# Differential attention: turning the weights of three pairs of heads by the DMA crossbar instead of by TensorE

## The chip, the cores and the metric

One Trainium2 chip; the kernel runs on one core. The metric is the device time of one execution in microseconds (us), as the median of several runs. The engines are named as in the profile: PE is TensorE (PEld its weight load), DVE VectorE, ACT ScalarE, POOL GpSimd, SP SyncE, which here issues the loads of weights.

## The reference

A hybrid decoder layer for 256 tokens of width 1024: a SwiGLU block, then a Mamba-2 branch and a branch of differential attention side by side, merged by gates, then a second SwiGLU block. What matters here is the attention, 8 heads in 2 blocks of 128 queries:

```
s = einsum('bqhmd,bkhmd->bhmqk', q_blk, k) * scale - slopes * dist      # m: two maps a head
s = where(dist >= 0, s, -inf)
p = softmax(s, axis=-1)
attn = p[:, :, 0] - lam * p[:, :, 1]
out = einsum('bhqk,bkhe->bqhe', attn, v)
out = rmsnorm(out, subln_g) * (1.0 - lam_init)
```

`attn` stands with the queries on the partitions. For the product with the values the keys have to be there, so each head's weights (three blocks of 128x128: the first queries with the first keys, the second queries with both) have to be turned.

## The kernel before

Float32 matmuls are made of a rounded part and its remainder: each 1 MB chunk of weights is loaded by SP into one of three buffers `raw`; ACT rounds it (`whi`, line 357, two halves a chunk) and DVE makes the remainder (`wlo`, line 358); when both halves are done, SP loads the next chunk into the buffer. PE multiplies whi and wlo with the tokens. Its order is written out by hand in this part: `natural` runs the products of the gates (`pgt`), of the Mamba-2 branch (`pws`) and of the attention (`pwd`) in blocks of 12 or 24 matmuls, and between two blocks lets a piece of `att_work` in, a generator that is measured out by microseconds and stops at each BREAK. The PSUM banks of these products (`pj`) are three that take turns; line 1847 (gates) or 1856 (`pws`) on DVE empties them. What stands on ACT and DVE is put in order by the scheduler, one row for each engine, worked off in that order.

`att_work` goes by waves of two heads, a pair. Wave n makes the scores of pair n on PE (`psc`), adds the distances on DVE (`s`, line 1625), takes the maximum (`nm`), exponentials on ACT (line 513, four a head) and combines the two maps on DVE (line 1647). In the same wave the pair before, n - 1, is turned: `Head.turn` puts three transposes a head on PE (`pa`, line 1653) and one copy on ACT (`aT`, line 1655). Then `values` multiplies aT with the values (`po`, lines 1665 to 1667), and `Pair.norm` makes the square (`o`, line 1679, ACT), its sum on DVE (`ro`, lines 1681 and 1682), its power by Ln and Exp on ACT, and the product (`o`, line 1686, DVE). A pair's result is turned a wave or so later (`pto`, line 1692, PE; `oh`, line 1704, ACT). Behind the third pair's softmax the gates' sigmoids (`gt`) stand on ACT between two loads of a table.

The tiles `s` come from a pool of four buffers (`k3`), `aT` and `o` from one of seven (`k2`). The second SwiGLU block already turns two tiles by DMA (`by_dma`, lines 1083 to 1090): ACT copies the low and the high 16 bits of each float apart, a DMA issued from ACT turns both planes, and ACT puts the halves together again.

Of the kernel before, what the change touches and what calls it, by code (L numbers as in the profile page):

```python
# [18 lines left out]
U16 = mybir.dt.uint16  # L19
# [8 lines left out]
P = 128  # L28
# [20 lines left out]
SSD_US = 1.55  # L49
DOWN = {"f1": "q1 Q2 q3 Q0 ppp", "f2": "q1 Q2 q3 Q0 ppp"}  # L50
DMA_TURNS = ("f2",)
WIDE_Z = ((0, 0), (1, 0), (1, 1))
FIRST, LAST = (1, 2, 3, 5, 7, 6, 4), (1, 6, 7, 2, 3, 5, 4)
MIXED = (1, 2, 6, 5, 3, 7, 4)
# [4 lines left out]
def tile_hybrid_layer(ctx: ExitStack, tc: tile.TileContext, x, ffn1_pre_g, ffn1_w_gate, ffn1_w_up,  # L59
# [4 lines left out]
    nc = tc.nc  # L64
# [8 lines left out]
    def k3(shape, name, dt=F32):  # L73
        return sb.tile(shape, dt, tag="k3", name=name, bufs=K3_BUFS)

    def k2(shape, name, dt=F32):
        return sb.tile(shape, dt, tag="k2", name=name, bufs=K2_BUFS)
# [15 lines left out]
    def bg(shape, name):  # L93
        return ps.tile(shape, F32, tag="bg", name=name, bufs=5)


    class Quad:
# [6 lines left out]
        def __init__(self, i, products, homes=None):  # L104
            self.i, self.sums, self.products, self.homes = i, {}, products, homes
            self.uses = [[p for p in products if p in (1, 5)], [p for p in products if p in (5, 7)],
                         [p for p in products if p in (2, 4)], [p for p in products if p in (3, 6, 7)]]
# [296 lines left out]
    def take(ahead=AHEAD):  # L404

        i = taken[0]
        taken[0] += 1
        split_to(ahead_of(i, ahead))
        (of, p), w = units[i], splits[i]
        splits[i] = None  # L410
        if p is not None:
            return w
        his, los = w
        nj = chunks[of][1][1] // 2
        return (lambda j: his[j // nj][:, j % nj, :], lambda j: los[j // nj][:, j % nj, :])
# [37 lines left out]
    def mm_w(dst, name, w, act, scale=None):  # L453

        for m in range(2):
            acc = pj(f"{name}{m}")
            for part in PARTS[m]:
                mm_part(acc, w, act, m, part, part == PARTS[m][0])
            taken_from(acc, dst[:, m, :], scale)

    def mm_runs(dst, name, w, act, n, wide=True):


        banks = [pj(f"{name}{m}") if n % 2 == 0 or not wide else bg([P, 512], f"{name}{m}") for m in range(2)]
        for part in PARTS[n % 2]:
            for m, acc in enumerate(banks):
                mm_part(acc, w, act, m, part, part == PARTS[n % 2][0])
                if part == PARTS[n % 2][1]:
                    taken_from(acc, dst[:, m, :])
# [69 lines left out]
    h = const.tile([P, 2, D], F32, name="h")  # L539
# [44 lines left out]
    for name, v in (("mx", mix_pre_g), ("f2", ffn2_pre_g),  # L584
                    ("ng", ssd_norm_g), ("cb", ssd_conv_b), ("sg", da_subln_g)):
        n = v.shape[1] // P
# [43 lines left out]
    def turn(b, q, src, g, to, name):  # L630

        pu = transposed(b, q, src, name)
        gained(pu, q, g, *to(q))
        return pu
# [195 lines left out]
    def sums_of(g, even, odd):  # L830


        bs = (slice(0, P), slice(P, T))
        v = k4([P, 4, 2, P], f"sv{g}")
        full = g in (0, 3)
        hi, lo = ((k4 if full else k3)([P, 4 if full else 3, 2, P], f"s{n}{g}", F32R) for n in "hl")
        more = None if full else k2([P, 2, 2, P], f"s4{g}", F32R)
        nc.vector.tensor_tensor(v[:, 0], even[:, :, bs[1]], odd[:, :, bs[1]], ALU.add)
        nc.vector.tensor_sub(v[:, 2], even[:, :, bs[0]], even[:, :, bs[1]])
        nc.vector.tensor_sub(v[:, 1], v[:, 0], even[:, :, bs[0]])  # L840
        nc.vector.tensor_sub(v[:, 3], odd[:, :, bs[0]], v[:, 1])
        if full:
            split(hi, lo, v)
            return tuple([x_[:, i] for i in range(4)] for x_ in (hi, lo))
        split(hi, lo, v[:, 0:3])
        split(more[:, 0], more[:, 1], v[:, 3])
        return ([hi[:, i] for i in range(3)] + [more[:, 0]], [lo[:, i] for i in range(3)] + [more[:, 1]])
# [127 lines left out]
    class Norm:  # L975
# [16 lines left out]
        def turn0(self, q):  # L992
            self.pus.append(turn(0, q, h[:, 0, halves[q]], self.g, self.to0, self.tag))
# [14 lines left out]
        def turn1(self, q):  # L1008
            turn(1, q, self.un[q], self.g, in_u(1), self.tag)
# [44 lines left out]
    def ffn(post_v, tag, ready, turned, then, products):  # L1054
# [50 lines left out]
        for j in range(2, FF // T):  # L1105
# [6 lines left out]
            mm_runs(sg, f"pg_{tag}{j}", take(), act_u, 0)  # L1112
            if tag in DMA_TURNS and j in (2, 3):
                for t in turns:
                    next(t)
            if j == 2:
                if tag not in DMA_TURNS:
                    for b in range(2):
# [10 lines left out]
            if j // 2 in QUADS[tag]:  # L1129
                if j % 2:  # L1130
                    sums[j // 2] = sums_of(j // 2, even, sg)
                else:
                    even = sg
            if first and (j == 3 or tag not in DMA_TURNS):
                sums[0] = sums_of(0, first[0][:, :2, :], first[0][:, 2:, :])
# [465 lines left out]
    ol = [None] * 2  # L1601
    blk = (slice(0, P), slice(P, 3 * P))

    class Head:


# [41 lines left out]

        def turn(self):

            pa = bg([P, 3 * P], f"pa{self.hd}")
            for i3 in range(3):
                nc.tensor.transpose(pa[:, i3 * P:(i3 + 1) * P], self.s[:, 0, i3 * P:(i3 + 1) * P], ident)
            self.aT = k2([P, 3 * P], f"aT{self.hd}")
            nc.scalar.copy(self.aT, pa)
            self.s = None

# [10 lines left out]

    class Pair:


        def __init__(self, hp):
            self.hp = hp
# [35 lines left out]
    def att_work():  # L1709

        pairs = [Pair(hp) for hp in range(H_ATT // 2)]
        heads = [Head(hd, pairs[hd // 2]) for hd in range(H_ATT)]
        for n in range(H_ATT // 2 + 2):
            here, old = heads[2 * n:2 * n + 2], heads[2 * n - 2:2 * n] if n else []
            for head in here:
                head.scores()
            for head in here:
                head.softmax()  # L1720
                yield 2.3
            for head in old:
                head.turn()
            if n == 3:
                pairs[0].turn()
                yield 0.8
            if old and opens:
                opens.pop()()
            for head in here:
                head.combine()  # L1730
                yield 1.3
            yield BREAK
            if old:
                for head in old:
                    head.values()
                pairs[n - 1].norm()
                if n == 4:
                    pairs[2].turn()
                yield 1.8
            if n == 5:  # L1740
                yield BREAK
            if n in (3, 5):
                pairs[n - 2].turn()
                yield 0.8
# [39 lines left out]
    for g in range(4):  # L1784
        sz[g] = k4([P, 4, T], f"sz{g}")
        for i in range(2):
            dst = sz[g][:, i * 2:i * 2 + 2, :]
            if (g, i) in WIDE_Z:
                mm_w(dst, f"pz{g}{i}", take(), act_u)
# [10 lines left out]
    for c in range(4):  # L1800
# [7 lines left out]
        back.run(QK_US)  # L1808

    back.add(att_work())  # L1810


# [148 lines left out]
```

## Time and profile before

| | |
|---|---|
| time, median of 3 runs | 723.69 us (723.62 to 723.75) |
| the profiled execution | 723.79 us, its span 722.1 us |
| busy PE, DVE, ACT | 99%, 89%, 68% of the span |
| granted TensorE clock | 0.998 |

Times in the profile are microseconds from the start of the span. "x6" is a count of instructions, and in brackets stands the idle time of the engine ahead of the row with what ended it. A chain of work is followed back from the last instruction over what released each one. The rows of a stretch give the busy time of each engine.

### The profile page before, as it was taken

To read this page: it belongs to the slowest core of one execution; us is meant where nothing else is said; L and a number is where in the kernel's file an instruction comes from. 1 tells how busy PE (TensorE), PEld (TensorE's weight loads), DVE (VectorE), ACT (ScalarE), POOL (GpSimd) and SP (SyncE) were. 2 spreads that over 40 slices of the span, in tenths; PEclk is the share of its full clock that TensorE was granted. 3 is DMA by queue.
4 is the path that set the end of the run, shared out by engine and by line. 5 is a ranking of instruction groups with operands and counts; after the bars stand their busy time and mean duration, and the time that the engine had idled before them with its cause. 6 is when DMAs were issued, how large, how long until landed. Compare 5 with 4: busy or idle time off the path is not lost.

```text
span 722.1 us, 10617 instructions
## 1 busy us (share of the span) xinstructions
PE 714.0 (99%) x3933; PEld 613.1 (85%) x3933; DVE 642.9 (89%) x994; ACT 489.5 (68%) x831; POOL 60.8 (8%) x110
## 2 busy tenths in 40 slices
PE   9999999999999999999999999999999999999996
PEld 7888888887888888899888788888888888888885
DVE  6899999999979999887996998789789599989996
ACT  5676666766856777879965577775667476477572
POOL 4401110000140000000000000000021010110000
PEclk9999999999999999999999999999999999999999
DMA  8969977877574467765564663464557678976861
GB/s 301 265 209 336 324 244 287 322 270 282 170 226 137 133 220 230 227 207 183 163 222 146 208 223 131 164 234 163 163 170 234 203 233 282 330 265 250 298 234 59
DMA packets 102324, 161.54 MB, mean 224 GB/s; under 512 B 5420, under 2 KB 71552, under 8 KB 101248
## 3 DMA queue, kind: packets, MB, share of 16 engines
q1 hardware_dynamic: 92880, 135.80, 56.5%
q0 software_dynamic: 6976, 24.00, 9.4%
q10 hardware_dynamic: 2416, 1.05, 0.6%
q8 instruction: 31, 0.51, 0.3%
q14 instruction: 21, 0.17, 0.1%
HBM read 150.85 MB, written 9.47 MB: 222 GB/s over the span
## 4 chain that ended last, share of the span: by engine, by line
PE 97%; DMA 1%; DVE 1%; ACT 0%; issue 0%; DVEq 0%; ACTq 0%
PE pup_f L439 14%; PE pg_f L439 14%; PE pxs L439 6%; PE pws L480 6%; PE pgt L480 6%; PE acc_f2p L937 5%; PE acc_f1p L937 4%; PE pbc L439 3%; PE pk L439 3%; PE pq L439 3%; PE pn_f L496 3%; PE pn_mx L480 3%; PE pwd L480 3%; PE pn_f L480 3%; PE pz L439 2%; PE acc_f2p L775 2%
## 5 line engine op out<-in xcount | busy, mean ns | idle before, releaser
L358 DVE TENSOR_TENSOR wlo<-raw,whi 128x1024 fp32r<-128x1024 f32 x204 | 244.5, 1227 | 18.3 <-ACT whi L357 17.7
L357 ACT CAST whi<-raw 128x1024 fp32r<-128x1024 f32 x204 | 206.7, 1049 | 17.6 <-DMA raw<-in_ffn_w_gate_dram 6.4
L439 PE MATMUL pup_f<-u_f,whi 128*128 128x512 f32 x288 | 68.7, 391 | 0.0
L439 PE MATMUL pg_f<-u_f,whi 128*128 128x512 f32 x288 | 68.2, 389 | 0.0
L439 PEld LDWEIGHTS pg_f<-u_f,whi 128*128 128x128 f32 x288 | 54.1, 188 | 11.2
L439 PEld LDWEIGHTS pup_f<-u_f,whi 128*128 128x128 f32 x288 | 52.9, 188 | 10.2
L439 PEld LDWEIGHTS pg_f<-u_f,wlo 128*128 128x128 f32 x288 | 36.9, 191 | 1.4
L439 PE MATMUL pup_f<-u_f,wlo 128*128 128x256 f32 x288 | 37.6, 283 | 0.0
L439 PE MATMUL pg_f<-u_f,wlo 128*128 128x256 f32 x288 | 37.4, 283 | 0.0
L439 PEld LDWEIGHTS pup_f<-u_f,wlo 128*128 128x128 f32 x288 | 35.8, 192 | 0.1
L480 PE MATMUL pgt<-whi,u_mx 128*128 128x512 f32 x128 | 33.1, 393 | 0.0
L418 ACT CAST gh_f<-sg_f 128x512 fp32r<-128x512 f32 x18 | 11.2, 621 | 32.2 <-DVE sg_f L1125 30.3
L160 DVE TENSOR_TENSOR wql<-raw,wqh 128x1024 fp32r<-128x1024 f32 x28 | 32.7, 1219 | 0.3 <-ACT wqh L159 0.3
L439 PE MATMUL pxs<-u_mx,whi 128*128 128x512 f32 x128 | 29.9, 390 | 0.0
L445 ACT COPY su_f<-pup_f 128x256 f32<-128x256 f32 x36 | 13.4, 372 | 22.2 <-PE pup_f L439 22.1
L480 PEld LDWEIGHTS pgt<-whi,u_mx 128*128 128x128 f32 x128 | 23.6, 188 | 5.3 <-issue 0.7
L439 PEld LDWEIGHTS pxs<-u_mx,whi 128*128 128x128 f32 x128 | 23.8, 188 | 4.8
L159 ACT CAST wqh<-raw 128x1024 fp32r<-128x1024 f32 x28 | 27.4, 1047 | 0.0
L134 ACT CAST wqh<-wt 128x1024 fp32r<-128x1024 f32 x16 | 16.9, 1054 | 14.9 <-DVE wt L126 13.6
L1438 DVE SCALAR_TENSOR_TENSOR xs<-xr,cols_b,xs 128x255 f32<-128x255 f32 (+2 forms) x48 | 20.4, 480 | 0.5 <-ACT xs L1435 0.3
L1533 DVE TENSOR_TENSOR E<-E,cbm 128x768 f32<-128x768 f32 x16 | 15.3, 955 | 6.3 <-ACT E L513 6.3
L513 ACT ACTIVATE s<-s,nm 128x128 f32<-128x128 f32 (+1 forms) x32 | 14.3, 447 | 9.3 <-DVE nm L1628 7.2
(498 smaller groups left out, 1698.2 us busy)
## 6 DMA issues: line engine op xcount, KB each, us to landing
raw<-in_w_in_dram SPq DMA_DIRECT2D x40, 1024.0 KB, 5.2
raw<-in_ffn_w_gate_dram SPq DMA_DIRECT2D x20, 1024.0 KB, 6.6
raw<-in_ffn_w_up_dram SPq DMA_DIRECT2D x20, 1024.0 KB, 6.0
raw<-in_ffn_w_down_dram SPq DMA_DIRECT2D x18, 1024.0 KB, 6.0
ws<-in_ffn_w_down_dram POOLq DMA_DIRECT2D x16, 512.0 KB, 6.9
sums_f<-ws POOLq DMA_DIRECT2D x16, 512.0 KB, 6.1
raw<-sums_f SPq DMA_DIRECT2D x8, 1024.0 KB, 6.7
raw<-in_ssd_w_branch_dram SPq DMA_DIRECT2D x8, 1024.0 KB, 4.9
```

The lines of the kernel that those rows point to most:

```text
L134: nc.scalar.copy(hi, src)
L159: nc.scalar.copy(hi, src)
L160: nc.vector.tensor_sub(lo, src, hi.bitcast(F32))
L357: last_cast[0] = behind(nc.scalar.copy(hi, r[:, js, :]), "cast").ins
L358: m = nc.vector.tensor_sub(lo, r[:, js, :], hi.bitcast(F32))
L439: nc.tensor.matmul(to, w_(j)[:, m * P:(m + 1) * P], x_(j), start=first and j == 0, stop=not first and j == KD - 1, skip_group_check=True)
L480: nc.tensor.matmul(acc, a(k0 + j), b(j), start=first and i == 0, stop=last and i == 11)
L496: nc.tensor.matmul(accs[b], x_(k0 + j), w_(j), start=first and j == 0 and w_ is wh and x_ is acts[b][0], stop=last and j == 3 and w_ is wl)
L775: nc.tensor.matmul(acc[b][q][:, cs] if to is None else to, x_[:, ts], w_(kt)[:, halves[q]][:, cs], start=to is not None and kt == 0 and x_ ...
L937: nc.tensor.matmul(bank[p], x_, w_, start=p not in begun, stop=last and p in (1, 5, 6, 7))
L1438: nc.vector.scalar_tensor_tensor(dst[:, m, s:], acc[:, m, :T - s], cw(3 - s, c), dst[:, m, s:], ALU.mult, ALU.add)
L1533: nc.vector.tensor_tensor(E, E, cbm[g].unsqueeze(1).to_broadcast([P, 2, 3 * P]), ALU.mult)
```

## The change

For pairs 0, 1 and 2 the transposes on PE and the copies out of PSUM go. Behind the combination of a pair `Pair.apart` copies the 16-bit halves of both heads' weights apart on ACT (`ap`, two copies of 128x768), and one DMA from ACT's queue turns twelve blocks of 128x128 into `al`. In the next wave `Head.turn` puts the halves together with one copy on ACT a head (`aT`, 128x768 halves). `ap` and `al` take buffers of the pool k3, in turn with `s`. Pair 3 stays as it was.

```
+DMA_PA = (0, 1, 2)
...
+    def words(t):
+        return t.bitcast(U16).rearrange("p (c h) -> p h c", h=2)
...
         def turn(self):
+            self.aT = k2([P, 3 * P], f"aT{self.hd}")
+            if self.pair.hp in DMA_PA:
+                nc.scalar.copy(words(self.aT), self.pair.lands[:, self.hd % 2])
+                return
             pa = bg([P, 3 * P], f"pa{self.hd}")
...
+        def apart(self, heads):
+            planes = k3([P, 2, 2, 3 * P], f"ap{self.hp}", U16)
+            for head in heads:
+                nc.scalar.copy(planes[:, head.hd % 2], words(head.s[:, 0, :]))
+                head.s = None
+            self.lands = k3([P, 2, 2, 3 * P], f"al{self.hp}", U16)
+            nc.scalar.dma_start_transpose(self.lands.rearrange("p i h (k q) -> p (i h k) q", q=P),
+                                          planes.rearrange("p i h k -> p (i h k)"))
...
             for head in here:
                 head.combine()
                 yield 1.3
+            if here and n in DMA_PA:
+                pairs[n].apart(here)
             yield BREAK
```

The scheduler puts ACT's row in another order with it. The numbers in the names tell buffers apart and differ between the two programs, and so do the line numbers (357, 513 and 1679 of before are 359, 515 and 1698 now). ACT behind the softmax of pair 0 (heads 0 and 1), before:

```order
L513 ACTIVATE s_4375,sm_4381<-s_4375,nm_4378 128x256
L357 CAST whi_4441<-raw_4265 128x1024
L357 CAST whi_4499<-raw_4320 128x1024
L357 CAST whi_4503<-raw_4320 128x1024
L357 CAST whi_4562<-raw_4399 128x1024
L513 ACTIVATE s_4485,sm_4491<-s_4485,nm_4488 128x128
```

and now:

```order
L515 ACTIVATE s_4375,sm_4381<-s_4375,nm_4378 128x256
L359 CAST whi_4441<-raw_4265 128x1024
L1685 COPY ap_4460<-s_4351 128x768
L1685 COPY ap_4460<-s_4375 128x768
L1688 DMA_TRANSPOSE al_4463<-ap_4460 128x12x128
L359 CAST whi_4504<-raw_4320 128x1024
L359 CAST whi_4508<-raw_4320 128x1024
L1659 COPY aT_4549<-al_4463 128x2x384
L1659 COPY aT_4551<-al_4463 128x2x384
L515 ACTIVATE s_4490,sm_4496<-s_4490,nm_4493 128x128 x2
```

The copies aT, which stood behind the softmax of pair 1, now stand ahead of it, two casts behind the DMA. ACT from the end of the sigmoids to the softmax of pair 3, before:

```order
L506 ACT_TABLE_LOAD
L357 CAST whi_4753<-raw_4570 128x1024
L357 CAST whi_4757<-raw_4570 128x1024
L357 CAST whi_4825<-raw_4652 128x1024
L357 CAST whi_4829<-raw_4652 128x1024
L357 CAST whi_4874<-raw_4697 128x1024
L1679 ACTIVATE o_4794<-po_4787 128x512
L513 ACTIVATE ro_4796<-ro_4796 128x4 x2
L513 ACTIVATE s_4814,sm_4820<-s_4814,nm_4817 128x128 x2
```

and now:

```order
L359 CAST whi_4747<-raw_4567 128x1024
L1685 COPY ap_4769<-s_4633 128x768
L359 CAST whi_4751<-raw_4567 128x1024
L1685 COPY ap_4769<-s_4680 128x768
L359 CAST whi_4824<-raw_4654 128x1024
L1688 DMA_TRANSPOSE al_4772<-ap_4769 128x12x128
L1698 ACTIVATE o_4793<-po_4786 128x512
L359 CAST whi_4828<-raw_4654 128x1024
L1659 COPY aT_4895<-al_4772 128x2x384
L1659 COPY aT_4897<-al_4772 128x2x384
L515 ACTIVATE ro_4795<-ro_4795 128x4
L515 ACTIVATE s_4813,sm_4819<-s_4813,nm_4816 128x128
```

Here too the copies aT come ahead of ro and of the softmax of pair 3, one square and one cast behind the DMA; one cast of five (whi of the third chunk) went behind the softmax. On PE the rows of pa are gone and nothing else moved; ahead of them stands the same product as behind.

More of the change, by code (lines that the diff above doesn't have):

```diff
@@ L51 @@
 DMA_TURNS = ("f2",)
+DMA_PA = (0, 1, 2)
+DMA_PTO = ()
 WIDE_Z = ((0, 0), (1, 0), (1, 1))
@@ L1653, in turn @@
                 nc.tensor.transpose(pa[:, i3 * P:(i3 + 1) * P], self.s[:, 0, i3 * P:(i3 + 1) * P], ident)
-            self.aT = k2([P, 3 * P], f"aT{self.hd}")
             nc.scalar.copy(self.aT, pa)
```

## The prediction

> **What bounds the kernel now.** I read the page first, for the engine that carries the end:
>
> ```profile
> PE 714.0 (99%) x3933; PEld 613.1 (85%) x3933; DVE 642.9 (89%) x994; ACT 489.5 (68%) x831; POOL 60.8 (8%) x110
> PE 97%; DMA 1%; DVE 1%; ACT 0%; issue 0%; DVEq 0%; ACTq 0%
> ```
>
> TensorE (PE) is busy for 99% of the span and 97% of the chain that ended last lies on it. So what leaves PE is worth its full time, provided PE doesn't begin to wait instead. The second view is the chain from 415 to 500 us, where the attention lies (columns: start, length, work):
>
> ```profile
> 430.47 0.66 PE pa L1653 x6
> ...
> 447.95 0.66 PE pa L1653 x6
> ...
> 468.15 0.66 PE pa L1653 x6
> 468.81 0.44 PE pto L1692 x4
> 469.24 8.19 PE pws L480 x36
> ...
> 485.38 0.22 PE po L1665 x2
> ...
> 492.66 0.44 PE pto L1692 x4
> ```
>
> These are the transposes of pairs 0, 1 and 2, six a pair, and what PE does behind them, without a gap. The third view is the stretch by waves, busy time of each engine:
>
> ```profile
> 421.00:436.00 15.00, 15.00 (x79) 12.06 (x78) 14.75 (x32) 10.01 (x24) 0.00 (x0) 1.00 0.66 225
> 436.00:453.00 17.00, 17.00 (x93) 14.13 (x92) 12.50 (x26) 13.53 (x30) 0.00 (x0) 1.00 0.43 162
> 453.00:470.00 17.00, 17.00 (x95) 14.21 (x94) 14.26 (x27) 13.09 (x30) 0.00 (x0) 1.00 0.36 134
> ```
>
> The columns are the stretch and its length, then PE, PEld, DVE and ACT. PE has no idle time at all; ScalarE (ACT) has 5.0, 3.5 and 3.9 us. ACT is the engine that gets the new work, and it feeds PE with the rounded weights (whi) and, through VectorE (DVE), with their remainders (wlo). So the question is whether 12.4 us of ACT idle time, much of it waits inside a softmax, holds what comes.
>
> **What goes.** Eighteen transposes leave PE: 3 x 0.66 = 1.97 us of the chain. That is the most the change can gain. The profiled execution took 723.79 us (span 722.1 and 1.7 around it), 0.10 above the median of 723.69; I apply the sum to the median, so the best case is 721.7. ACT also loses six copies out of PSUM.
>
> **What comes, and its price.** The kernel already turns two tiles this way in the second feed-forward block, so most prices have a row:
>
> ```profile
> L1084 ACT COPY gp_f<-sg_f2b x2: 1047/1048/1049, 565.9 to 568.4; 128x1024 uint16<-128x1024 uint16 x2
> L1085 ACTq DMA_TRANSPOSE gt_f<-gp_f x2: 1247/1286/1324, 567.0 to 569.4; - x2
> L1089 ACT COPY g_f<-gt_f x2: 1360/1370/1380, 576.2 to 578.5; 128x1024 uint16<-128x1024 uint16 x2
> DMA to landing us min/median/max: 2.8/3.3/3.8
> L1655 ACT COPY aT<-pa x8: 458/468/486, 433.6 to 483.2; 128x384 f32<-128x384 f32 x8
> ```
>
> - A copy that takes the words apart (ap) has 768 halves against 1024: by size 0.79 us, at most 1.05. I take 0.8, two a pair.
> - A copy that puts them together (aT from al) is 1370 x 0.75 = 1.03; I take 1.0, two a pair.
> - The two copies that go took 0.84 a pair. Net, ACT gets 3.6 - 0.8 = 2.8 us more a pair, 8.4 in all.
> - The DMA issue holds ACT's queue for 1.25 to 1.32 us for eight blocks of 128x128. Here there are twelve: 1.3 if the price is fixed, 1.9 if it goes with the blocks. I take 1.6.
> - Landing, from the start of the issue: 2.8 and 3.8 us for eight blocks. Scaled wholly by size the mean of 3.3 gives 4.95; with the issue (1.29) left as it is and the rest scaled, 1.29 + 1.5 x 2.0 = 4.3. The low end is 3.3 (the quicker one, 2.8, plus half a microsecond for four more blocks), the high end 5.7 (3.8 x 1.5). I take 4.5, because the transposes are issued beside loads of weights:
>
> ```profile
> 423.69 0.37 SPq L339 DMA_DIRECT2D raw<-in_ssd_w_branch_dram  x1
> raw<-in_ssd_w_branch_dram SPq DMA_DIRECT2D x8, 1024.0 KB, 4.9
> ```
>
> This 1 MB load is issued at 423.69, within half a microsecond of the first new transpose as worked out below. The Trainium skill (Advanced Engine Details and Errata, X-Bar Transpose (TRN2)) says that such transposes run as fast as ordinary DMAs and expects 350 to 400 GB/s. By that 384 KB would be an estimated 1.0 us of transfer, which leads to the first rival. Against the change speaks the skill's VectorE: DVE Perf Modes, The three transpose paths: 1309 ns for a 128x128 block by DMA and 390 ns by TensorE. Taken one behind another, twelve blocks would be 15.7 us, three times 11 us more than I use, and the time about 759; the trace doesn't bear that out, since eight blocks landed in 2.8 to 3.8 us.
>
> **Where ACT waits for the landing.** ACT's instructions stand in one row, and in the new order the copies aT of a pair stand ahead of the softmax of the next pair, with only two whi (first wave) or the square o and one whi (second and third) between the DMA issue and them. ACT rows of before that I need:
>
> ```profile
> 427.82 0.40 ACT L513 ACTIVATE s<-s,nm 128x128 f32<-128x128 f32 x1 [1.98 <-DVE nm L1628]
> 433.60 0.83 ACT L1655 COPY aT<-pa 128x384 f32<-128x384 f32 x2
> 435.27 2.01 ACT L357 CAST whi<-raw 128x1024 fp32r<-128x1024 f32 x2 [0.84 <-PE pgt L480]
> 437.97 0.60 ACT L1679 ACTIVATE o<-po 128x512 f32<-128x512 f32 x1 [0.69 <-PE po L1667]
> 442.54 0.40 ACT L513 ACTIVATE s<-s,nm 128x128 f32<-128x128 f32 x1 [1.62 <-DVE nm L1628]
> 446.30 1.04 ACT L357 CAST whi<-raw 128x1024 fp32r<-128x1024 f32 x1
> 454.61 4.83 ACT L357 CAST whi<-raw 128x1024 fp32r<-128x1024 f32 x5
> 461.96 0.44 ACT L513 ACTIVATE ro<-ro 128x4 f32<-128x4 f32 x2 [2.02 <-DVE ro L1682]
> 470.12 3.90 ACT L357 CAST whi<-raw 128x1024 fp32r<-128x1024 f32 x4
> 478.78 1.05 ACT L357 CAST whi<-raw 128x1024 fp32r<-128x1024 f32 x1 [0.67 <-PE po L1667]
> 482.80 0.84 ACT L1655 COPY aT<-pa 128x384 f32<-128x384 f32 x2
> ```
>
> and of DVE and SyncE (SP):
>
> ```profile
> 421.79 0.75 DVE L1647 SCALAR_TENSOR_TENSOR s<-s,c 128x128 f32<-128x128 f32 x2
> 424.78 1.01 DVE L1625 SCALAR_TENSOR_TENSOR s<-dneg,psc 128x384 f32<-128x384 f32 x2
> 434.54 0.75 DVE L1647 SCALAR_TENSOR_TENSOR s<-s,c 128x128 f32<-128x128 f32 x2
> 462.43 0.69 DVE L1686 TENSOR_TENSOR o<-po,ro 128x512 f32<-128x512 f32 x1
> 464.43 0.68 DVE L1856 TENSOR_TENSOR gt<-pws,gt 128x512 f32<-128x512 f32 x1
> 473.72 0.37 SPq L339 DMA_DIRECT2D raw<-in_da_w_branch_dram  x1
> ```
>
> From these, a whi costs 1.0 us and the eight exponentials of a pair 3.8 (442.54 to 446.30).
>
> Wave 1. Pair 0 is combined at 422.5 (421.79 + 0.75). Second ap to 423.4, issue to 425.0, two whi to 427.0, landing 423.4 + 4.5 = 427.9, so ACT idles 0.9; two aT to 429.9. The softmax of pair 1 starts there instead of at 427.82, and with its 3.8 us and two whi ends at 435.7, not 433.60: 2.1 late.
>
> Wave 2. The combination ended 1.7 behind the last exponential (435.3 against 433.6), so now at 437.4. Second ap to 438.2, issue to 439.8, o and whi to 441.3, landing 442.7 (1.4 idle), aT to 444.7, ro 0.5, exponentials to 449.0 against 446.30. From there to the whi at 454.61 stood 8.3 us with the tables, the gates' sigmoids and two aT; without the aT 7.6, so 456.6, 2.0 late.
>
> Wave 3. Two whi and two ap to 460.2, issue to 461.8, o and whi to 463.3, landing 464.7 (1.4 idle), aT to 466.7, ro to 467.2 where it ended at 462.4, exponentials and two whi to 473.0, oh 0.6: the whi of 470.12 starts at 473.6, 3.5 late.
>
> **What that does to PE.** Two things hang on it. First, behind ro stand on DVE o (0.69) and gt (0.68), which empties the PSUM bank that PE wants for the second block of rows of the next pws (three banks take turns): free at 468.6, wanted at 469.24 - 1.97 = 467.3, a wait of 1.3 us. Second, a chain runs without slack from the whi at 470.12 over their wlo, the load that SP issues at 473.72 when a buffer is free, the whi of that load at 478.78 and ro to aT of pair 3, which ended at 483.6; its reader po stood at 485.38. Moved by 3.5 it ends at 487.1, while PE comes at 485.38 - 1.97 = 483.4: 3.7 us, 1.3 of which PE has then already spent. The last pto follows po at an unchanged distance and adds nothing. Sum: -1.97 + 3.7 = +1.7 us, 725.4.
>
> Costed at nothing: the first ap of waves 1 and 2 (beside DVE's combination, else 0.8 each), the wait of the next pair's tiles s, which now need the buffers that the ap copies empty (these end at 423.4, DVE writes s from 424.78), DVE's changed order.
>
> How the sum hangs on the landing: the idle times 0.9, 1.4 and 1.4 shrink with it, one for one, and each wave starts where the last ended, so a microsecond on all three landings moves the end by three. At 3.3 us the sum is 1.7 - 3.3 = -1.6 (722.1), at 5.7 it is 1.7 + 3.6 = +5.3 (729.0). Zero lies at 3.9.
>
> **Rivals.**
> 1. Faster: the landings are short, about 3.1 to 3.4 us, as the second transpose of the row above (2.8) was with no load beside it. Then ACT's waits vanish, the 12.4 us of idle time hold the 8.4 us of copies and the issues, and PE keeps its 1.97 us: 721.7 to 722.2. It decides below 3.4. The skill's bandwidth would put it here. Against it: eight blocks took 3.8 once, and loads stand beside all three.
> 2. No change: landings of 3.4 to 4.4 us give back about what PE gains, 722.3 to 725.1.
> 3. Much slower: the transposes' packets wait behind the loads of 1 MB, landing then at 5.7 or later, with these loads' own 4.9 as its scale: 729 and more.
> 4. That the change doesn't take the transposes off PE: excluded by the order of instructions.
>
> **How the numbers follow.** This measurement can tell about 0.2%, 1.45 us, from no change. Landings above 4.4 us (slower; the forecast and rival 3): 0.52, of which rival 3 has 0.10. Between 3.4 and 4.4: 0.26. Below: 0.22. The forecast's own range is 725.1 to 728.6; with the faster and the equal cases the range is 722.0 to 728.6.
>
> **What would show it.** Right: no pa of pairs 0 to 2 on PE; 2.8 us more ACT work a pair; ACT idle before aT and released by the DMA; idle time of PE before a pws near 467 released by DVE, and before po near 484 released by ACT. Wrong: landings near 3 us with ACT never idle before aT; or an aT that isn't ahead of the softmax in time; or PE waiting at pws for wlo, which would mean that the weights themselves come late.

## The result and the profile after

The changed kernel takes 730.91 us (median of 6 runs, 729.53 to 733.86) against 723.65 beside it on the same chip: ratio 1.0104, 95% interval 1.0088 to 1.0121. It is 7.3 us slower, in the direction that was forecast and by four times the amount; 725.4 was predicted, with 728.6 as the end of the range. The profiled execution took 733.2 us (span 731.4). In what follows, medians are of all runs of a kernel; the ratios and their intervals are worked out from the single runs and can differ from the quotient of two medians by 0.1%.

The page of the changed kernel, busy time of the engines and the chain that ended last:

```profile
PE 714.5 (98%) x3915; PEld 611.9 (84%) x3915; DVE 643.3 (88%) x994; ACT 496.3 (68%) x837; POOL 60.4 (8%) x110
...
PE 81%; DVE 6%; DMA 5%; ACT 4%; issue 2%; SPq 0%; DVEq 0%; ACTq 0%
```

PE lost its 18 transposes (3933 to 3915 instructions), and ACT is busy for 6.8 us more (8.4 were forecast). But PE carries 81% of the chain, not 97. The chain from 415 to 505 us says where the rest went (start, length, work):

```profile
423.47 7.07 DMA al<-ap
431.50 1.04 ACT aT L1659
...
440.91 6.18 DMA al<-ap
447.12 1.98 ACT aT L1659 x2
...
463.73 7.06 DMA al<-ap
470.81 1.94 ACT aT L1659 x2
...
473.33 0.69 DVE o L1705
474.02 0.60 DVE gt L1877
```

All three transposes stand on it, 20.3 us together, where PE stood before. Behind the third come the two aT, the end of ro on ACT, and on DVE o and the gt that empties the PSUM bank for pws. The tiles ap and al in the trace (durations in ns: least, median, most), and the waits between 415 and 500 us (who <- for whom: total, times, longest):

```profile
L1685 ACT COPY ap<-s x6: 822/828/833, 421.6 to 462.9; 128x768 uint16<-128x768 uint16 x6
...
L1659 ACT COPY aT<-al x6: 1028/1048/1068, 430.6 to 471.7; 128x768 uint16<-128x768 uint16 x6
L1688 ACTq DMA_TRANSPOSE al<-ap x3: 1485/1516/1669, 423.5 to 463.7; - x3
...
DMA to landing us min/median/max: 6.2/7.1/7.1
```

```profile
ACT aT L1659 <- DMA al<-ap: 10.4, 3, 4.0
...
DVE o L1705 <- ACT ro L515: 6.1, 3, 3.3
```

Copies and issue cost what was set for them. The landings took 6.2 to 7.1 us instead of 4.5, ACT idled 10.4 us before aT instead of 3.7, and DVE's o waited 6.1 us for ro; the longest of these three waits, 3.3 us, is that of the third wave, with gt behind it. The stretches (length; busy PE, PEld, DVE, ACT, POOL; granted PE clock; DMA share; GB/s) show that PE still runs without a gap in the second wave (and in the first) and that the loss falls in and behind the third:

```profile
436.00:453.00 17.00, 17.00 (x90) 14.08 (x89) 13.76 (x31) 12.81 (x36) 0.00 (x0) 1.00 0.67 147
453.00:470.00 17.00, 14.26 (x79) 11.60 (x77) 10.26 (x17) 13.13 (x14) 0.00 (x0) 1.00 0.47 147
470.00:486.00 16.00, 11.32 (x45) 9.34 (x46) 12.71 (x25) 13.97 (x29) 0.00 (x0) 0.79 0.44 144
```

The last of these stretches in the kernel before:

```profile
470.00:486.00 16.00, 16.00 (x86) 13.67 (x85) 12.42 (x17) 11.24 (x17) 0.00 (x0) 1.00 0.78 264
```

The clock is new too: 0.79 in that stretch, 1.00 before. PE's instructions behind its wait (start, length):

```profile
474.68 2.08 PE L482 MATMUL pws<-whi,yh 128*128 128x512 f32 x4 [7.42 <-DVE gt L1877]
476.55 1.91 PE L482 MATMUL pws<-wlo,yh 128*128 128x512 f32 x4
478.26 1.47 PE L482 MATMUL pws<-whi,yl 128*128 128x512 f32 x4
479.57 1.08 PE L482 MATMUL pws<-whi,yh 128*128 128x512 f32 x4
```

From start to start, four matmuls took 1.87, 1.71 and 1.31 us, and then 0.92. The twelve slow ones cost 4.89 - 3 x 0.92 = 2.1 us.

With PE's own waits this is nearly the whole account of the profiled execution. The waits in the whole span, first after, then before:

```profile
PE pws L482 <- DVE gt L1877: 7.4, 1, 7.4
PE warm L576 <- DVE zeros L555: 1.1, 1, 1.1
PE pu_f L1179 <- DMA h<-in_x_dram: 0.9, 2, 0.7
PE pto L1711 <- DVE o L1705: 0.6, 1, 0.6
PE po L1674 <- ACT aT L1664: 0.4, 1, 0.4
```

```profile
PE warm L574 <- DVE zeros L553: 1.1, 1, 1.1
PE acc_f1p L775 <- DVE wlo L358: 0.5, 1, 0.5
PE pu_f L1177 <- DMA h<-in_x_dram: 0.2, 1, 0.2
```

Waits 10.4 against 1.8 make +8.6, the clock +2.1, the transposes that went -1.97: +8.7 of the 9.3 us between the spans (731.4 and 722.1).

That is PE's account of its own time. By the chain of this execution the clock's 2.1 us did not move the end: from the gt at 474.02 to 501.66 us no instruction of PE stands on it, but the load and the casts on which aT of pair 3 hangs, and PE, slower clock and all, still came too early to po of that pair (two pieces of the chain, and PE's row):

```profile
482.50 1.23 DVE wlo L360
483.75 5.45 DMA raw<-in_da_w_branch_dram
```

```profile
493.56 0.49 PE L1674 MATMUL po<-v,aT 128*128 128x128 f32 x2 [0.43 <-ACT aT L1664]
```

At the full clock PE would, by this chain, have waited some 2.5 us there instead of 0.4.

### The profile page after: what moved, and what is told of

It is laid out like the page before. It is cut to its first block, busy times and chain, and to the rows that moved or that the text cites. A ratio compares the mean times of both kernels' runs of the same rounds, so it can differ in the third digit from the quotient of the medians.

```text
span 731.4 us, 10589 instructions
## 1 busy us (share of the span) xinstructions
PE 714.5 (98%) x3915; PEld 611.9 (84%) x3915; DVE 643.3 (88%) x994; ACT 496.3 (68%) x837; POOL 60.4 (8%) x110
## 4 chain that ended last, share of the span: by engine, by line
PE 81%; DVE 6%; DMA 5%; ACT 4%; issue 2%; SPq 0%; DVEq 0%; ACTq 0%
PE pup_f L441 14%; PE pg_f L441 14%; PE pxs L441 6%; PE acc_f1p L939 5%; PE pbc L441 3%; PE pk L441 3%; PE pq L441 3%; PE pn_mx L482 3%; PE pwd L482 3%; PE pn_f L482 3%; PE pn_f L498 3%; DMA al<-ap 3%; PE pgt L482 3%; PE pz L441 2%; PE acc_f1p L777 2%
## 5 line engine op out<-in xcount | busy, mean ns | idle before, releaser
L482 PE MATMUL pws<-whi,yh 128*128 128x512 f32 x64 | 18.7, 415 | 7.4 <-DVE gt L1877 7.4
```

The costliest lines, as they stand in the source:

```text
L482: nc.tensor.matmul(acc, a(k0 + j), b(j), start=first and i == 0, stop=last and i == 11)
```

## Experiments

The theory: the landing is long because each transpose shares the DMA engines with a 1 MB load of weights, and it costs because ACT, whose instructions stand in one row, waits for it ahead of ro and of the next softmax. Against it stood that ACT's added work is what costs; that the transposes hold up the weights; and that twelve blocks take this long by themselves.

**Without the wait, and without the DMA**

The first reads the planes in place of the landing; the DMAs still run, and aT stays ahead of the next softmax by an added order. The second drops the DMAs as well; it has no added order, and its trace shows the aT copies ahead of the next softmax all the same (423.19 and 425.05 us, the first exponential at 427.87).

```
-  nc.scalar.copy(words(self.aT), self.pair.lands[:, self.hd % 2])
+  nc.scalar.copy(words(self.aT), self.pair.planes[:, self.hd % 2])
...
-  self.lands = k3([P, 2, 2, 3 * P], f"al{self.hp}", U16)      # second run only
-  nc.scalar.dma_start_transpose(...)                           # second run only
```

> The changed kernel, but the two aT copies of each of the three pairs read the 16-bit planes and not the transposes' landing, so ScalarE waits for no landing there; the copies, the planes, the three DMA transposes and their issue stay (the weights of these pairs are then not turned). Theory (the wait): ScalarE's idle 3.3, 3.1 and 4.0 us before aT are what costs the time; without them 721.7 to 723.5 us, PE's wait at pws under 1 us. Rival (the work): the added copies and the issue of some 1.6 us a pair on ScalarE cost it, not the wait; then 728 to 731 us. Rival (the contention): the transposes hold up the weight loads and PE waits for these; then also above 727 us, with PE or DVE waiting behind raw.

> As the run without the wait, but the three DMA transposes are not issued at all (the weights of the three pairs are not turned). Theory (the wait): within 1 us of the run without the wait, 721.5 to 723 us, since the issue of 1.5 to 1.7 us stands where ScalarE has slack. Rival (the issue on ScalarE's queue or the packets' share of the DMA engines): 2 us or more below the run without the wait.

Measured: 721.75 us without the wait (before: 723.42; ratio 0.9976, 0.9962 to 0.9989) and 721.47 without the DMA (0.9970, 0.9961 to 0.9979). In the run without the wait the transposes landed even later than in the changed kernel:

```profile
L1693 ACTq DMA_TRANSPOSE al<-ap x3: 1509/1530/1683, 422.6 to 458.0; - x3
...
DMA to landing us min/median/max: 7.1/8.6/8.8
```

Nobody waited for them, and the nine microseconds were gone. So a late landing by itself, its share of the DMA engines, and the issue of 1.5 us on ACT's queue cost nothing that can be told here; the two runs differ by 0.3 us. The copies, 6 x 0.83 + 6 x 1.05 us less six that went, are hidden. The wait is the price of this kernel. And the gain was right: 1.97 us were worked out for PE, and without the DMA the medians differ by 1.95 (the interval reaches from 1.5 to 2.8).

**aT behind the next softmax**

```
-  nc.scalar.copy(words(self.aT), self.pair.lands[:, self.hd % 2])
+  m = nc.scalar.copy(words(self.aT), self.pair.lands[:, self.hd % 2])
+  tc.add_manual_dep(m.ins, act_last[0].name, order, ...)
```

> The changed kernel with one edit: on ScalarE the aT copies of a pair stand behind the last exponential of the next pair, not ahead of its first. Landings stay as they are. Theory (the wait, by its place): 6 to 7 us of landing pass beside the next pair's softmax, ScalarE idles less than 0.5 us before aT, DVE's ro is not late, PE waits at pws less than 1.5 us: 721.7 to 724 us, which may be below the kernel before. Rival (the work): 728 us and more, since not one instruction is taken from ScalarE. Third way: the aT copies now come too late for po, and PE waits at po 1 us or more in each wave: 725 to 729 us.

Measured: 724.72 us (before 723.42; ratio 1.0024, 1.0008 to 1.0040). ACT has no wait for the landing left, and six of the seven microseconds are back, but the time lies above the 721.7 to 724 us of the theory. What happened is nearest the third way, in one wave instead of each and at a smaller price. PE's waits of this run:

```profile
PE po L1675 <- ACT aT L1665: 1.6, 1, 1.6
PE pto L1712 <- DVE o L1706: 1.0, 1, 1.0
```

The aT that po waits for is that of pair 3, which TensorE turns: in the third wave the two copies now stand ahead of six whi, and behind these are the load, its whi, ro and that aT, the second chain of the prediction.

This run also has a landing without company. The second wave's transposes were issued at 438.7, 2.3 us ahead of the next load (DMA queues between 438 and 443 us; the 185 packets that the loads moved in these 5 us lie before the transposes' first packet or behind their last):

```profile
q10 hardware_dynamic: 1568, 0.39, 35.4%
...
al<-ap ACTq DMA_TRANSPOSE x1, 3.2
```

3.2 us for the same twelve blocks, against 7.1 in the first wave of the same run, where a load was issued 0.3 us behind them. (In the third, with a load 0.5 us behind, nobody waited and the landing isn't in the trace; the last packets moved 6.2 us after the issue.) Twelve blocks don't take long by themselves.

**Twelve blocks elsewhere**

```
+  nc.scalar.copy(planes[:, :1024], sgs[1].bitcast(U16))
+  nc.scalar.copy(planes[:, 1024:], sgs[1].bitcast(U16)[:, :512])
+  nc.scalar.dma_start_transpose(lands..., planes)
```

> The kernel before with one DMA transpose of twelve blocks more, whose result nobody reads, issued by ScalarE in the second feed-forward block ahead of the two of eight blocks (two copies on ScalarE make its source). There a weight load runs for its first part only. Theory (twelve blocks beside a 1 MB load land late, alone they don't): 3.4 to 4.5 us from issue to landing where the queue carries nothing else, 1 to 3 us more for each stretch that it shares with the load. Rival (twelve blocks take so long by themselves): 6 to 7 us with or without a load. The time of this kernel decides nothing.

Measured: landing 8.2 us. The place was badly chosen: between 559 and 571 us the loads moved 3069 packets beside it, from a load issued 3.3 us and another 0.5 us ahead.

```profile
q1 hardware_dynamic: 3069, 3.09, 76.3%
...
alq<-apq ACTq DMA_TRANSPOSE x1, 8.2
```

So it says nothing on twelve blocks alone; the landing of 3.2 us above does.

**The transposes on SP's queue, ahead of the load**

```
-  nc.scalar.dma_start_transpose(self.lands...
+  nc.sync.dma_start_transpose(self.lands...
```

> The changed kernel with the three transposes issued by SP, each ahead of the weight load that ran beside it, in place of ScalarE; aT stays ahead of the next softmax. Theory (twelve blocks land late because a 1 MB load is on the DMA engines with them): landing 3.2 to 4.0 us, as the one that met no load in the run with aT behind the softmax (3.2 us); ScalarE idles under 1 us a pair before aT; 721.5 to 724 us. Rival (the loads pay instead): the loads come 3 us later, the casts of raw wait for them, and PE waits at pws or po all the same: 726 to 730 us. Rival (twelve blocks take 6 to 7 us by themselves): landings unchanged, 729 to 732 us.

Measured: 724.73 us (before 723.93; ratio 1.0011, 0.9993 to 1.0029): aT stays ahead of the next softmax, only the queue differs in the program (the scheduler now puts ro between the two copies in the second and third wave), and 6 us are back, though the time is above the 721.5 to 724 us expected. The transposes in the chain of this run, and ACT's wait for them:

```profile
423.30 3.32 DMA al<-ap
...
437.01 4.19 DMA al<-ap
...
458.46 4.45 DMA al<-ap
```

```profile
ACT aT L1659 <- DMA al<-ap: 5.4, 3, 2.1
```

The landings are short, as the theory says (two of them a little over the 4.0 expected), and PE doesn't wait for the loads behind them (its waits in the attention are 0.9 us at pto, 0.4 at pws and 0.3 at po). ACT's idle time before aT, 5.4 us in place of 10.4, is more than the "under 1 us a pair" expected: the issue no longer fills 1.5 us of ACT's time between the planes and aT, so ACT comes to aT earlier.

Why the load beside it matters is seen in the packets. From 427.0 to 428.5 us in the changed kernel (queue: packets, MB, share), both queues have work:

```profile
q1 hardware_dynamic: 256, 0.52, 90.0%
q10 hardware_dynamic: 242, 0.06, 18.1%
```

They go about one for one, but a packet of the load carries 2 KB and one of the transposes 256 bytes. The transposes move 242 packets in 1.5 us; with the same queue ahead of the load they had the engines alone and moved at (GB/s in 40 slices from 424.9 to 426.5 us, 1264 packets):

```profile
GB/s 288 282 294 288 288 301 288 282 294 288 288 301 288 282 294 288 288 301 288 282 294 288 282 301 275 256 193 212 103 84 167 102 51 51 0 0 0 0 0 0
```

The Trainium skill (DMA: Bandwidth & Descriptors, Queues, rings and completion order) says that each DMA engine takes turns between the queues it has work for, packet by packet; 256 against 242 agrees with it. The 350 to 400 GB/s that the Trainium skill expects of such transposes (Advanced Engine Details and Errata, X-Bar Transpose (TRN2)) were not reached: 282 to 301 alone, and 0.06 MB in 1.5 us, 40 GB/s, beside a load.

Taking turns is not the whole of the long landings. Alone, the first packet moved 1.2 us after the issue (438.74, 439.93 in the run with aT behind the softmax). So it did in the third wave of the changed kernel, and there a whole load, 512 packets of 2 KB, went between the transposes' packets. In the first wave no packet of the transposes moved from the issue at 423.47 to 426.9 us; the only queue in the rows of that stretch is the loads':

```profile
q1 hardware_dynamic: 219, 0.42, 48.2%
```

In the second wave they stood still for 2 us in the middle (last section). Why they stand still is open; that it takes a load is what the landings of 3.2 us show. Nor is it the queue by itself: in the run with both remedies, below, the transposes of the second wave were issued by SP 0.5 us behind a load (437.20 and 437.66 us) and landed after 7.5 us.

**Only the first two pairs**

Once as in the change, once with aT behind the softmax: `DMA_PA = (0, 1)`.

> The changed kernel with the third pair turned by TensorE again; the first two as in the change. Theory (each wave's wait is passed on to PE in full): the third wave's idle 4.0 us goes, the first two waves' 3.3 and 3.1 us stay: 5 to 6 us over the run without the DMA, 726.5 to 729 us. Rival (only the third wave, where PE waits for po and pws, costs): 722 to 724 us.

> aT behind the next pair's last exponential, and only the first two pairs turned by DMA; the third goes by TensorE as before. With all three so placed PE ran without a wait through the first two waves and lost 2.6 us in and after the third (PE busy 14.45 of 16.0 and 12.99 of 14.0 us in the stretches from 470 and 486 us), where ScalarE's two copies stand ahead of six casts that the loads and ro wait for. Theory (each wave pays for itself): the loss goes with the third pair and two times 0.66 us of PE are gained: 721.9 to 722.9 us, below the kernel before. Rival (the two copies a pair, of 1.05 us, end in the same place whichever pair they belong to): 723.5 to 725 us.

Measured: 727.63 us for the first (before 723.93; ratio 1.0047, 1.0030 to 1.0064). The third wave's own idle time is gone, the waits of the first two waves (3.3 and, with a landing of 3.8 in the second, 0.7 us) still reach PE, which waits 1.6 us at pws and 1.7 at po. So a wave passes its lateness on, as the prediction had it, and that of the first two, 3.3 of the 4.0 us from the first, is enough for a slowdown. That the time lies in the range expected is in part luck: the range was worked out from 3.3 and 3.1 us of waits, and the second measured 0.7. In the second run the copies aT stand behind the softmax: 723.38 us (ratio 0.9991, 0.9972 to 1.0010). No wait at po is left and PE is idle for 0.4 us from 421 to 500 us; the time lies between the ranges of the theory and of its rival, and the interval holds both a gain and no change, so no gain is shown. The trace does bear out that the loss of 724.72 us sat with the third wave's copies: PE is busy for 16.00 of the 16 us from 470 us, where it had 14.45. The second landing of this run, again with no load in its flight, took 3.2 us, as the one above.

**Both remedies**

The copies of a pair stand behind the exponentials of the first head of the next pair, and the transposes go on SP's queue. The second run leaves them on ACT's.

```
   for head in here:
       head.softmax()
+      if head is here[0]:
+          first_exp[0] = act_last[0].name
...
+  tc.add_manual_dep(m.ins, first_exp[0], order, ...)
...
-  nc.scalar.dma_start_transpose(self.lands...      # first run only
+  nc.sync.dma_start_transpose(self.lands...        # first run only
```

> Both remedies at once: the three transposes issued by SP, each ahead of the weight load beside it, and each pair's aT copies on ScalarE behind the exponentials of the first head of the next pair, among or ahead of those of the second. Theory (the wait of an in-order ScalarE for the landing is the whole price): landings of 3.3 to 4.5 us pass beside 2 to 4 us of other ScalarE work, idle before aT under 0.3 us, ro is no longer behind aT, and the copies stand early enough for po: 721.3 to 722.7 us, as the run without the DMA, below the kernel before. Rival (the two copies, wherever they stand, put casts and ro late in the third wave): 723.5 to 725 us, as the two remedies apart.

> As the run with both remedies, but the transposes stay on ScalarE's queue, so they run beside a load again. Theory: landings of 6 to 7 us in the first and third wave, 4 to 5.5 us in the second; in the two long ones ScalarE idles 1.5 to 3 us before aT, now with ro and one head's softmax already done: 722.5 to 725.5 us, 1 to 3 us above the run with both remedies. Rival (the place alone cures it): within 0.5 us of the run with both.

Measured: with both, 722.96 us (before 723.74; ratio 0.9977, 0.9962 to 0.9992), faster than the changed kernel by 8 us and than the kernel before by little: 0.8 us by the medians, a little short of the 721.3 to 722.7 expected. On ACT's queue at the same place: 725.05 (ratio 1.0009, 0.9991 to 1.0026). With both remedies no instruction of ACT waits for a landing, though the one that SP issued behind a load took 7.5 us, and from 421 us on PE runs without a gap up to 486 us:

```profile
470.00:486.00 16.00, 16.00 (x91) 13.84 (x91) 15.42 (x26) 13.31 (x25) 0.00 (x0) 1.00 0.77 275
```

On ACT's queue all three landings take 6.9 to 7.2 us and ACT idles only 0.64 us for them; I had expected 1.5 to 3. Another 1.1 us of ACT's time in the third wave goes behind the issue. The casts on which the next load hangs start 0.7 us later than with both remedies (473.06 and 472.39 us), the copies to aT of pair 3 1.1 us later (483.93 and 482.83), and PE waits 2.0 us at po (timelines of ACT and of PE):

```profile
461.63 1.05 ACT L359 CAST whi<-raw 128x1024 fp32r<-128x1024 f32 x1 [1.09 <-issue]
...
466.97 1.07 ACT L1661 COPY aT<-al 128x768 uint16<-128x768 uint16 x1 [0.64 <-DMA al<-ap]
```

```profile
484.44 0.49 PE L1677 MATMUL po<-v,aT 128*128 128x128 f32 x2 [1.95 <-ACT aT L1667]
```

So the place alone doesn't cure it: 2.1 us lie between the two medians. The trace is of an execution of 723.46 us, the fastest of the ten and only 0.5 us over the profiled one with both remedies, so it shows where ACT and PE wait, but not the whole difference. That in the third wave, where a chain without slack follows, the issue on ACT costs part of it is argued from these rows; no run separates it from the wait of 0.64 us.

## Why the prediction failed

- The bound, the gain and the added work were right. PE at 99% was what mattered, the gain of 1.97 us was measured as 1.95 (1.5 to 2.8), the copies at 0.83 and 1.05 us stood for 0.8 and 1.0, the issue at 1.5 to 1.67 for 1.6.
- The step that failed is the landing, taken as 4.5 us "because the transposes are issued beside loads of weights", with 5.7 (3.8 x 1.5) as the high end. It measured 7.1, 6.2 and 7.1. The mean of two landings of eight blocks was scaled by size, and the load beside them went into it as a few tenths. Yet in the kernel before the two rows of eight blocks, 2.8 and 3.8 us, already differed by a third without a difference in size. What sets the landing is whether loads are on the DMA engines with it: 3.2 us without, 6.2 to 7.1 with, by taking turns with the load's packets and, in the first two waves, by some 2 us of standing still.
- "A microsecond on all three landings moves the end by three" held in the profiled execution. The landings were 2.6, 1.7 and 2.6 us over 4.5, together 6.8; 725.4 + 6.8 = 732.2, against a median of 730.9 and 733.2 in the profiled execution. ACT's idle times 0.9, 1.4 and 1.4 became 3.3, 3.1 and 4.0.
- The places of the waits were right, near 467 us for gt and at po of pair 3 for aT, and so was the chain to po. Predicted were 1.3 us at pws and 2.4 more at po. With 6.7 us more of lateness the same sum gives 8.0 at pws and again 2.4 at po, and po at 483.4 + 3.7 + 6.7 = 493.8 us. Found were 7.4 at pws, then 2.1 us of lowered clock and 0.4 at po, which started at 493.56.
- Rival 3 is what happened in landing and time: packets held up by the loads, 5.7 us or later, 729 and more. It had a chance of 0.10 and lay outside the range, which ended at 728.6 although the prediction's own high end of the landing, 5.7 us, gave 729.0. Its scale, the load's own 4.9 us, stood in the prediction, and so did a load issued within half a microsecond of the first transpose.
- Not foreseen at all was the clock. It cost PE 2.1 us in the profiled execution, in time that PE would, by the chain, have waited at po anyway.
- Costed at nothing and rightly so, as far as it shows: the first ap, the tiles in k3, DVE's changed order. The transposes' share of the DMA engines had no term at all. The run with all of these and without the wait is faster than before, by 0.24% (0.11 to 0.38).

## What to carry over

The DMA that an in-order engine waited for was priced here by what else was on the DMA engines, more than by its size: look up which large loads are issued shortly before it or within its flight. Here loads put 3 to 4 us on top of a landing of 3.2 in the changed kernel, and up to 5.6 in the run without the wait, of the size of a load's own 4.9 us. Ahead of the load on the same queue the landings took 3.3 to 4.5 us. Put the instruction that consumes it behind work that would have run anyway, and look for what stands behind it in the same row of instructions, since a wait there delays engines that have nothing to do with the transfer. Here either remedy gave back some 6 of 7 us, and only both together turned the loss into a small gain: 0.23% by the single runs (0.08 to 0.38), 0.8 us by the medians, less than half of what leaving the DMA out shows to be there.

## What the runs showed of the hardware

- Packets of two queues of 2 KB and of 256 bytes alternated about one for one (256 against 242 in 1.5 us), so the small ones got 40 GB/s beside the large ones and some 288 alone.
- A queue with work can stand still while another moves next to nothing. In the second wave of the changed kernel the transposes, issued at 440.9 and begun at 442.1, moved not one packet between 443.1 and 445.1 us, while the queue of the loads moved 25 packets in the same 2 us. This is the only queue in the rows of that stretch:

```profile
q1 hardware_dynamic: 25, 0.05, 6.6%
```

  Why the transposes stand still is not settled; no run was made for it.
- After a long wait PE runs at a lower clock for a while. Stretches of the changed kernel around the wait that began at 467.3:

```profile
467.00:472.00 5.00, 0.26 (x3) 0.02 (x1) 3.04 (x6) 1.19 (x2) 0.00 (x0) 1.00 0.81 264
472.00:478.00 6.00, 3.32 (x8) 2.66 (x9) 4.67 (x9) 5.42 (x18) 0.00 (x0) 0.52 0.33 126
478.00:480.00 2.00, 2.00 (x8) 1.58 (x7) 2.00 (x8) 2.00 (x6) 0.00 (x0) 0.73 0.00 0
480.00:486.00 6.00, 6.00 (x32) 5.11 (x31) 6.00 (x10) 5.36 (x6) 0.00 (x0) 1.00 0.66 209
```

  The granted clock fell to 0.52 some 5 us into the wait and was at 1.00 again by 480, some 5 us after its end at 474.7. Behind PE's waits of 1.6 to 2.0 us in the experiments it stayed at 1.00. The Trainium skill (TensorE: Matmul & The Clock Gate, Part 1: The HAM clock gate) has the clock halved after an idle window of about 3.4 us and full again after one busy window; the rows agree as far as they go: a wait of 7.4 us was long enough, waits of up to 2.0 were not, and none between was met.
